# A decoder block on one core: the mixer's splits on VectorE with held rows, candidate sums on GpSimd, the output projection's first tiles side by side, and an ordered norm

## The chip, the cores and the metric

The kernel runs on one core of a Trainium2 chip. The engines have the profile's names: PE is TensorE, DVE is VectorE, ACT is ScalarE, POOL is GpSimd, and SP is SyncE, which here only issues transfers. The metric is the device time of one execution in microseconds, as the median of several runs. The kernel before takes 1098.89 us.

## What is computed

One decoder block on 256 tokens (T) of width 1024 (D), in float32:

```
mod = silu(c) @ w_ada + b_ada              # 6 x 1024: shift1, scale1, gate1, shift2, scale2, gate2
hn  = modulate(rmsnorm(x, norm1_g), shift1, scale1)
qa, ka, va, qi, ki, wi, qb, kb, vb, ga, gb = split(hn @ w_in)
ya  = dsa_attention(qa, ka, va, qi, ki, wi, rel_bias)      # indexer, top 64 keys, softmax
yb  = stick_breaking_attention(qb, kb, vb)
merged = sigmoid(ga) * (ya @ w_proj_a) + sigmoid(gb) * (yb @ w_proj_b)
x   = x + gate1 * (merged @ w_out)
h   = modulate(rmsnorm(x, norm2_g), shift2, scale2)
# peer_ffn: 8 heads; s1, s2 = the top 16 of 128 keys on either half
cand = s1[..., :, None] + s2[..., None, :]                 # candidate sums
top_s, pos = top_k(cand, 16);  g = softmax(top_s)
f   = sum_k g_k * gelu(h . u[e_k]) * v[e_k]
out = rmsnorm(x + gate2 * f, final_g)
```

## The kernel before

**One stream of weights.** A class `Stream` (L58) carries every weight matrix as tiles of 128 x 1024, 512 KB each, in one list `items`: 16 pieces of w1, 29 of w2 (both are w_in), 4 of wpa, 4 of wpb, 8 of wout, 16 of wq, 128 of u and 128 of v. For each piece SP's queue loads `raw` (L78), ACT copies it to `wh` in the reduced format fp32r (L96), and one subtraction raw - wh gives the rest `wl` (L102). That subtraction is called the split. PE multiplies in three products (`three`, L256 to L259): wh with the activations' high part, wh with their low part, wl with the high part. `raw` runs at most 3 pieces ahead (`RAW_AHEAD`) and the splits 2 (`SPLIT_AHEAD`). The third entry of an item says who splits: DVE, POOL, or, where it is None, POOL while `S.share` holds and DVE after that. In the five matrices w2 to wq every odd piece (`i % PS`) goes to POOL, and all of wq.

```
items.append(("mat", A[nm][i], None if nm == "wq" else nc.gpsimd if i % PS else V))
while late and (32 - len(late)) * (45 - VEC0) < 32 * (k - VEC0):
    items.append(late.pop(0))
```

**Rows of the modulation.** The 48 rows of w_ada come in the same list as items of kind "vec": each is loaded as `vraw` by SP's queue and reduced against `cond` by one DVE instruction (L143). 16 are used by the first norm; the other 32 are "late" and are spread over 45 pieces from w2 to wout. They have a pool of three buffers.

**The order.** A scheduler fixes each engine's order at build time from the order of the program and the data dependences. `tc.issue_after(x)` adds the rule that an instruction comes behind instruction x. A late row has no such rule, so it can be moved forward as far as its load allows.

**Mixer.** While the w2, wpa and wpb pieces run, a generator `attention()` adds a step after each piece: the indexer with its top-k on DVE (L420 to L433), the softmax attention and the stick-breaking attention (the DVE results lg L481, lb and lm L536 and L537, ll L541; PE's tiles `at`). Its bias table `brev` is a 1 MB load on POOL's queue (L390), which ACT and POOL then split in two halves (L443, L444). `psm` holds two accumulators "mm".

**Output projection and norm.** Each wpb piece gives m, mh and the rest ml (L662 to L665: two DVE operations, an ACT copy, a DVE subtraction). Then the 8 wout pieces run one after the other: x2 is updated (L679), ACT squares it (L681), POOL sums the squares (L683), and two matmuls with ones (L685) give the norm's sum, then Ln (L234), Exp (L237). Transposes of x2 (L706) save the residual through ACT copies (L708) to DRAM.

**Top-k.** During the 16 wq pieces a head's scores are copied to `s` every second piece (L940), and `topk()` on DVE takes the top 16 of each half (`top16`, L745 to L749: MAX8, FIND_INDEX8, MATCH_REPLACE8, MAX8, FIND_INDEX8). After heads 3 and 7 it adds candidate sums (L796, L798) and takes their top 16. Then e = TV - max (L812), Exp on ACT (L833), lookups, index tables `ix` (L778), three PE transposes `tp` each for the two halves of the tokens (L857). The generators are advanced by budgets: each `yield` names a cost, and a piece grants a number.

**Experts.** 128 u pieces with a Gelu each (L963), while `gates()` on DVE and PE builds the gate matrix; then 128 v pieces; then the last norm.

## Time and profile before

| | before |
|---|---|
| median of 3 runs | 1098.89 us (1098.52 to 1099.18) |
| the profiled execution's own time | 1098.71 us |
| span of its instructions | 1097.0 us |
| busy: PE, DVE, ACT, POOL | 1038.3, 788.4, 576.4, 151.6 us |
| mean granted clock of PE | 0.982 |

The span runs from the first to the last instruction of the execution; its own time has 1.7 us around that. A busy time is the sum of an engine's instructions; PE's is 95% of the span, so 58.7 us are left in which PE does nothing. A row of the profile names line, engine, operation and tiles (out<-in); "[idle before <-releaser]" is the time that the engine stood before it and whose result ended that.

### The profile page before, as it was taken

Reading aid. Unit: us, or ns where it says so; the run is one execution under the profiler, and the core shown is the slowest. Engines: PE = TensorE matmul, PEld = TensorE weight load, DVE = VectorE, ACT = ScalarE, POOL = GpSimd, SP = SyncE. Lnnn points to the kernel's source line nnn. Section 1 sums busy time; section 2 is a strip of 40 time slices with the busy share of each in tenths; the row PEclk is TensorE's granted clock in tenths of the full one; section 3 lists DMA queues with packets and bytes.
Section 4 is the critical chain, followed back from the end, with each engine's and each line's share of the span. In section 5 each row is a group of like instructions: output and inputs, shape, how many; then the busy total and the mean of one; then the engine's idle time right before and its main releaser. Section 6 shows DMA issues by size and latency. Waiting matters only on the chain.

```text
span 1097.0 us, 18990 instructions
## 1 busy us (share of the span) xinstructions
PE 1038.3 (95%) x7237; PEld 952.6 (87%) x7237; DVE 788.4 (72%) x1510; ACT 576.4 (53%) x938; POOL 151.6 (14%) x88
## 2 busy tenths in 40 slices
PE   6997888998994999999999999999999999999996
...
GB/s 299 361 357 216 253 244 133 176 153 195 165 153 101 152 183 172 154 155 173 155 155 167 153 163 183 183 185 241 222 195 195 192 192 192 193 193 193 193 194 72
DMA packets 57949, 208.50 MB, mean 190 GB/s; under 512 B 6673, under 2 KB 6785, under 8 KB 57858
## 3 DMA queue, kind: packets, MB, share of 16 engines
...
q10 hardware_dynamic: 240, 0.08, 0.0%
...
## 4 chain that ended last, share of the span: by engine, by line
PE 80%; DVE 12%; issue 3%; POOL 2%; ACT 1%; DMA 1%; SPq 0%; POOLq 0%; ACTq 0%; DVEq 0%
PE acc L1035 31%; PE mm L257 13%; PE mm L259 13%; PE mm L258 13%; PE gp L897 3%; DVE vraw L143 2%; POOL wl L102 2%; PE a L258 2%; PE a L257 2%; PE a L259 1%; DMA vraw<-in_ada 1%; DVE tmp L747 1%; DVE ll L541 1%; DVE wl L102 1%; DVE cand L798 1%
## 5 line engine op out<-in xcount | busy, mean ns | idle before, releaser
L102 DVE TENSOR_TENSOR wl<-raw,wh 128x1024 fp32r<-128x1024 f32 x285 | 353.1, 1239 | 182.2 <-ACT wh L96 182.1
L96 ACT ACTIVATE wh<-raw 128x1024 fp32r<-128x1024 f32 x333 | 352.9, 1060 | 247.8 <-PE mm L258 144.4
L257 PE MATMUL mm<-hh,wh 128*128 128x256 f32 x1304 | 376.3, 289 | 12.1 <-ACT Xlo L963 9.1
L259 PE MATMUL mm<-hh,wl 128*128 128x256 f32 x1304 | 371.6, 285 | 4.3 <-DVE wl L102 3.6
L258 PE MATMUL mm<-hl,wh 128*128 128x256 f32 x1304 | 371.7, 285 | 0.1
L257 PEld LDWEIGHTS mm<-hh,wh 128*128 128x128 f32 x1304 | 252.6, 194 | 13.7 <-ACT Xlo L963 9.3
L259 PEld LDWEIGHTS mm<-hh,wl 128*128 128x128 f32 x1304 | 252.4, 194 | 4.8 <-DVE wl L102 3.8
L258 PEld LDWEIGHTS mm<-hl,wh 128*128 128x128 f32 x1304 | 252.9, 194 | 0.6 <-issue 0.3
L1035 PE MATMUL acc<-wh,cl 128*128 128x512 f32 x500 | 154.0, 389 | 0.0
L1035 PE MATMUL acc<-wh,ch 128*128 128x512 f32 x500 | 153.9, 389 | 0.0
L1035 PE MATMUL acc<-wl,ch 128*128 128x512 f32 x500 | 153.9, 389 | 0.0
L102 POOL TENSOR_TENSOR wl<-raw,wh 128x1024 fp32r<-128x1024 f32 x48 | 122.5, 2557 | 165.7 <-ACT wh L96 165.7
L1035 PEld LDWEIGHTS acc<-wh,cl 128*128 128x128 f32 x500 | 93.8, 188 | 19.5
L1035 PEld LDWEIGHTS acc<-wl,ch 128*128 128x128 f32 x500 | 93.8, 188 | 19.4
L1035 PEld LDWEIGHTS acc<-wh,ch 128*128 128x128 f32 x500 | 93.8, 188 | 19.5
L1065 POOL TENSOR_TENSOR Xlo<-Xlo 128x512 f32<-128x512 f32 x3 | 3.8, 1282 | 728.5 <-DVE Xlo L1062 727.8
L983 ACT ACTIVATE ch<-Xhi 128x256 fp32r<-128x256 f32 x80 | 33.4, 418 | 96.4 <-PE acc L1035 96.4
L143 DVE CUSTOM_DVE_ANT_0 vraw<-vraw,cond,par 128x1024 f32<-128x1024 f32 x48 | 72.1, 1507 | 2.7 <-DMA vraw<-in_ada 2.7
L985 DVE TENSOR_TENSOR cl<-Xhi,ch 128x256 fp32r<-128x256 f32 x80 | 34.0, 425 | 38.3 <-PE acc L1035 38.3
L983 ACT ACTIVATE ch<-Xlo 128x256 fp32r<-128x256 f32 x48 | 19.9, 418 | 52.9 <-PE acc L1035 52.9
L909 ACT ACTIVATE Xhi<-gp 128x640 f32<-128x640 f32 (+21 forms) x32 | 18.6, 582 | 43.5 <-DVE Xhi L905 42.0
L257 PE MATMUL a<-hh,wh 128*128 128x256 f32 x128 | 34.9, 293 | 3.3 <-ACT hh L252 3.3
...
## 6 DMA issues: line engine op xcount, KB each, us to landing
raw<-in_u SPq DMA_DIRECT2D x128, 512.0 KB, 3.6
raw<-in_v SPq DMA_DIRECT2D x128, 512.0 KB, 4.2
vraw<-in_ada SPq DMA_DIRECT2D x48, 512.0 KB, 5.0
raw<-in_w SPq DMA_DIRECT2D x45, 512.0 KB, 4.8
raw<-in_wq SPq DMA_DIRECT2D x16, 512.0 KB, 3.6
raw<-in_wout SPq DMA_DIRECT2D x8, 512.0 KB, 3.6
raw<-in_wpa SPq DMA_DIRECT2D x4, 512.0 KB, 4.4
raw<-in_wpb SPq DMA_DIRECT2D x4, 512.0 KB, 3.6
```

The source lines that it names most:

```text
L96: self.marka.append(nc.scalar.activation(h, raw, AF.Copy).ins)
L102: ins = arg.tensor_sub(l, raw, h.bitcast(F32)).ins
L143: vins[j] = nc.vector.tensor_tensor_reduce(raw, raw, cond, 1.0, par[:, j:j + 1], OP.mult, OP.add, accum_out=mod[:, j:j + 1]).ins
L257: nc.tensor.matmul(ps, wh, xh, start=start, stop=False, **k)
L258: nc.tensor.matmul(ps, wh, xl, start=False, stop=False, **k)
L259: nc.tensor.matmul(ps, wl, xh, start=False, stop=stop, **k)
L541: nc.vector.tensor_sub(ll, lm, lh.bitcast(F32))
L897: nc.tensor.matmul(gp[:, k], o1[:, k // 2, :, k % 2], o2[q][:, k // 2, :, k % 2], start=q == 0, stop=q == 1)
L909: nc.scalar.activation(t[:, m:, ts], g[:, a + m:a + n], AF.Copy, scale=1.0 / GS)
L983: nc.scalar.activation(ch, c, AF.Copy)
L985: nc.vector.tensor_sub(cl, c, ch.bitcast(F32))
L1035: nc.tensor.matmul(accs[tt * 2 + half], a[:, ts], b[:, half * 512:(half + 1) * 512], start=i == 0 and k == 0, stop=i == 127 and k == 2, sk ...
```

## The change

1. All splits of w2, wpa, wpb, wout and of the first three wq pieces are on DVE (`PS` is gone). The late rows begin after 8 pieces (`VEC0` 8) and each is held behind DVE's last split (`self.low`).
2. The load of `brev` moves from POOL's queue to SP's, and the two copies of it lose one of their two rules of order.
3. The last wpb piece makes m, mh and ml in two halves; the first two wout pieces are multiplied side by side, k 0 to 5 of both, then k 6 and 7 of both.
4. In the norm the transposes of x2's first half stand ahead of the two sums on PE, two of their copies ahead of Ln on ACT, the rest behind Exp.
5. The candidate sums are on POOL, in buffers of their own; their top 16 stand behind all heads in program order. `S.share` ends with the second candidate set. Both Exps stand together; the transposes (`turn`) come later.

```diff
-VEC0 = 0
-PS = 2
+VEC0 = 8
...
         if kind == "vec":
-            arg(raw)
+            with tc.issue_after(self.low) if i >= 4 * ND else nullcontext():
+                arg(raw)
...
-            if arg is nc.gpsimd:
-                self.mark.append(ins)
+            if arg is nc.vector:
+                self.low = ins
...
-            items.append(("mat", A[nm][i], None if nm == "wq" else nc.gpsimd if i % PS else V))
+            items.append(("mat", A[nm][i], None if nm == "wq" and i > 2 else V))
...
-        with tc.issue_after(S.mark[-1]):
-            nc.gpsimd.dma_start(brev, bass.AP(tensor=brow[:].tensor, offset=brow[:].offset,
...
+        nc.sync.dma_start(brev, bass.AP(tensor=brow[:].tensor, offset=brow[:].offset,
...
+        for a, b in ((0, 1), (1, 2)) if i == 3 else ((0, 2),):
+            f = lambda t, j: t[:, j + a:j + b].rearrange("p a b -> p (a b)")
+            c = slice(a * T, b * T)
+            nc.vector.tensor_mul(m[:, c], o[:, c], f(gate[1], 2 * i))
+            nc.vector.tensor_add(m[:, c], m[:, c], f(m1, 2 * i))
+            nc.scalar.activation(f(mh, 2 * i), m[:, c], AF.Copy)
+            nc.vector.tensor_sub(f(ml[i // 2], 2 * i % 4), m[:, c], f(mh, 2 * i).bitcast(F32))
...
+    two = [(S.next(), mm()) for _ in range(2)]
+    for ks in (range(6), range(6, ND)):
+        for (wh, wl), o in two:
+            for k in ks:
+                three(o[:, :T], wh[:, k * P:(k + 1) * P], wl[:, k * P:(k + 1) * P], mh[:, k], mlk[:, k], k == 0,
+                      k == ND - 1)
...
+    turned(0, 0, 0)
+    turned(1, 1, 0)
+    for j in (0, ND - 1):
+        on_pe(ss[:, :T], ones, sq[:, j], start=j == 0, stop=j > 0)
...
+    turned(2, 0, 4, exp)
+    turned(3, 1, 4, exp)
...
-                    cand = tw.tile([P, 4, NC], F32, name="cand")
+                    cand = tk.tile([P, 4, NC], F32, name=f"cand{h}{tt}")
-                    nc.vector.tensor_tensor(cand[:, :, :16], v1[:, :, 0:1].to_broadcast([P, 4, 16]), v2, op=OP.add)
+                    nc.gpsimd.tensor_tensor(cand[:, :, :16], v1[:, :, 0:1].to_broadcast([P, 4, 16]), v2, op=OP.add)
-                        nc.vector.tensor_tensor(
+                        nc.gpsimd.tensor_tensor(
...
-                    for k in range(4):
-                        top16(cand[:, k], NC, TV[tt][:, h - 3 + k], TP[tt][:, h - 3 + k])
-                        yield 950
+                    cands.append((cand, tt, h - 3))
+        for n, (cand, tt, h) in enumerate(cands):
+            S.share = n < 2
+            for k in range(4):
+                top16(cand[:, k], NC, TV[tt][:, h + k], TP[tt][:, h + k])
+                yield 980
...
-        S.share = False
...
-            if tt == 0:
+            if tt:
+                turn(0)
+            else:
                 for a in es:
                     nc.scalar.activation(a, a, AF.Exp)
...
+        yield 3000
+        turn(1)
```

What this does to the engines' orders shows at three places. The first is DVE in the mixer, in the second half of the indexer's top-k (MAX and MATCH_REPLACE; `ISA vraw,mod` is a late row, `wl` a split). Before:

```order
L429 MATCH_REPLACE ism<-m_1176,ism 128x128 [waits DVE_49]
L143 ISA vraw,mod<-vraw,cond,par 128x1024 [waits DMAHW0_49]
L143 ISA mod 128x1
L428 MAX m_1176<-ism 128x8 [waits DVE_49]
L143 ISA vraw,mod<-vraw,cond,par 128x1024 [waits DMAHW2_49]
L143 ISA mod 128x1
L429 MATCH_REPLACE ism<-m_1176,ism 128x128 [waits DVE_49]
L102 TENSOR_TENSOR wl<-raw,wh 128x1024 [waits DMAHW7_49,Activation_49]
L428 MAX m_1176<-ism 128x8 [waits DVE_49]
L143 ISA vraw,mod<-vraw,cond,par 128x1024 [waits DMAHW4_49]
```

and in the change, at the same steps:

```order
L102 TENSOR_TENSOR wl<-raw,wh 128x1024 [waits DMAHW0_49,PE_49,Activation_49]
L428 MATCH_REPLACE ism<-m_1161,ism 128x128 [waits DVE_49]
L143 ISA vraw,mod<-vraw,cond,par 128x1024 [waits DMAHW2_49]
L143 ISA mod 128x1
L427 MAX m_1161<-ism 128x8 [waits DVE_49]
L102 TENSOR_TENSOR wl<-raw,wh 128x1024 [waits DMAHW1_49,Activation_49]
L428 MATCH_REPLACE ism<-m_1161,ism 128x128 [waits DVE_49]
L143 ISA vraw,mod<-vraw,cond,par 128x1024 [waits DMAHW4_49]
L143 ISA mod 128x1
```

Before, several rows stand between two splits; now each split is followed by one row, and the splits are twice as many.

The second place is POOL from the wq pieces on (`wl` a split, `cand` a candidate sum). Before it holds splits alone here:

```order
L239 TENSOR_TENSOR xr_2482<-xr_2482,rr 128x256
L700 DMA gscr<-gr 8x128
L710 DMA xscr<-xts 128x512 x4
L734 DMA sk_2863<-in_sk 128x1024
L734 DMA sk_2864<-in_sk 128x1024
L102 TENSOR_TENSOR wl<-raw,wh 128x1024 x23
L1065 TENSOR_TENSOR Xlo<-Xlo 128x512 x3
```

and in the change the sums of heads 0 to 3 and 4 to 7 stand between the splits:

```order
L102 TENSOR_TENSOR wl<-raw,wh 128x1024 x9
L836 TENSOR_TENSOR cand_3345<-V_2871,V_2873 128x4x24
L836 TENSOR_TENSOR cand_3345<-V_2871,V_2873 128x4x48
L834 TENSOR_TENSOR cand_3345<-V_2871,V_2873 128x4x16
L836 TENSOR_TENSOR cand_3349<-V_2872,V_2874 128x4x24
L836 TENSOR_TENSOR cand_3349<-V_2872,V_2874 128x4x48
L102 TENSOR_TENSOR wl<-raw,wh 128x1024
L834 TENSOR_TENSOR cand_3349<-V_2872,V_2874 128x4x16
L102 TENSOR_TENSOR wl<-raw,wh 128x1024 x6
L836 TENSOR_TENSOR cand_3739<-V_2871,V_2873 128x4x24
L836 TENSOR_TENSOR cand_3739<-V_2871,V_2873 128x4x48
L834 TENSOR_TENSOR cand_3739<-V_2871,V_2873 128x4x16
```

The sums of one token half of four heads are three instructions. On DVE the first MAX over a candidate set now waits for POOL, at this place behind the fourth head (V and I are heads' results, TV and TP those of candidates):

```order
L770 MAX_INDEX I_2878<-V_2874,s_3284 128x8 [waits DVE_49]
L773 MAX_INDEX I_2876<-V_2872,tmp 128x8 [waits DVE_49]
L771 MATCH_REPLACE tmp<-V_2874,s_3284 128x128
L769 MAX TV_2879<-cand_3345 128x8 [waits Pool_49]
L772 MAX V_2874<-tmp 128x8 [waits DVE_49]
L770 MAX_INDEX TP_2881<-TV_2879,cand_3345 128x8 [waits DVE_49]
L773 MAX_INDEX I_2878<-V_2874,tmp 128x8 [waits DVE_49]
L769 MAX TV_2879<-cand_3345 128x8 x2
L770 MAX_INDEX TP_2881<-TV_2879,cand_3345 128x8 [waits DVE_49] x2
L769 MAX TV_2879<-cand_3345 128x8
L769 MAX TV_2880<-cand_3349 128x8 [waits Pool_49]
```

The scheduler has moved the first halves of the candidates' top 16 up to here; the rest of them stands behind the last head.

The third place is ACT around the Exps, at the fourth and fifth u piece (Xlo is the Gelu of a piece). Before:

```order
L963 ACTIVATE Xlo<-mm 128x256
L833 ACT_TABLE_LOAD
L833 ACTIVATE e<-e 128x128
L96 ACTIVATE wh<-raw 128x1024
L963 ACT_TABLE_LOAD
L963 ACTIVATE Xlo<-mm 128x256
L833 ACT_TABLE_LOAD
L833 ACTIVATE e<-e 128x128
L963 ACT_TABLE_LOAD
L963 ACTIVATE Xlo<-mm 128x256
```

and in the change:

```order
L996 ACTIVATE Xlo<-mm 128x256
L96 ACTIVATE wh<-raw 128x1024
L996 ACTIVATE Xlo<-mm 128x256
L874 ACT_TABLE_LOAD
L874 ACTIVATE e<-e 128x128 x2
L996 ACT_TABLE_LOAD
L996 ACTIVATE Xlo<-mm 128x256
```

There are two table loads fewer, and both Exps stand behind the fifth Gelu in place of the fourth and fifth.

## Rows read from the trace of the kernel before

**Rows 1.** The page: PE's busy time with its share of the span and its instructions (part 1), and the groups of DVE's splits and ACT's copies (part 5: count, busy us and mean ns of one, then idle time before them).

```profile
PE 1038.3 (95%) x7237; PEld 952.6 (87%) x7237; DVE 788.4 (72%) x1510; ACT 576.4 (53%) x938; POOL 151.6 (14%) x88
...
L102 DVE TENSOR_TENSOR wl<-raw,wh 128x1024 fp32r<-128x1024 f32 x285 | 353.1, 1239 | 182.2 <-ACT wh L96 182.1
L96 ACT ACTIVATE wh<-raw 128x1024 fp32r<-128x1024 f32 x333 | 352.9, 1060 | 247.8 <-PE mm L258 144.4
```

**Rows 2.** The waits of PE over the span: line, released by which engine's tile and line, us in total, times, longest us.

```profile
PE mm L257 <- ACT Xlo L963: 9.1, 1, 9.1
PE tp L857 <- DVE ix L778: 5.0, 1, 5.0
PE mm L610 <- POOL wl L102: 4.9, 1, 4.9
PE mm L259 <- DVE wl L102: 3.6, 1, 3.6
...
PE at L551 <- DVE ll L541: 3.1, 3, 1.5
PE mm L257 <- ACT hh L252: 2.8, 1, 2.8
...
PE mm L257 <- ACT mh L664: 2.1, 2, 1.1
PE at L685 <- POOL sq L683: 1.9, 1, 1.9
```

**Rows 3.** Six windows: us, then busy us (and count) of PE, PE's weight loads, DVE, ACT and POOL, PE's granted clock, DMA share, GB/s.

```profile
97.62:101.04 3.42, 3.42 (x19) 3.42 (x18) 3.42 (x12) 0.00 (x0) 1.61 (x2) 0.50 0.88 302
111.28:118.10 6.82, 5.91 (x14) 4.65 (x15) 6.82 (x10) 0.76 (x1) 4.17 (x2) 0.50 0.54 168
172.72:176.13 3.41, 3.41 (x19) 3.19 (x17) 3.18 (x6) 3.38 (x6) 0.00 (x0) 0.50 0.76 293
234.16:240.98 6.82, 6.18 (x29) 6.18 (x30) 2.14 (x3) 3.23 (x4) 2.21 (x2) 0.50 0.26 79
343.38:350.21 6.83, 2.87 (x13) 2.87 (x14) 6.83 (x21) 5.80 (x7) 3.00 (x1) 0.50 0.10 13
353.62:360.45 6.83, 3.72 (x18) 3.75 (x19) 6.83 (x15) 0.00 (x0) 2.81 (x2) 0.50 0.51 154
```

**Rows 4.** The same columns for stretches of the mixer, and for that of the output projection and its norm (235 to 262).

```profile
62.00:105.00 43.00, 39.39 (x248) 34.06 (x248) 41.60 (x76) 22.46 (x34) 18.59 (x9) 0.96 0.77 278
105.00:150.00 45.00, 37.10 (x245) 31.65 (x244) 42.01 (x94) 22.48 (x46) 19.59 (x8) 0.92 0.76 257
150.00:195.00 45.00, 39.68 (x311) 34.08 (x309) 38.05 (x76) 33.39 (x63) 9.60 (x4) 0.96 0.51 175
...
235.00:262.00 27.00, 25.09 (x187) 24.63 (x188) 7.39 (x12) 12.84 (x19) 20.24 (x13) 0.89 0.54 155
```

**Rows 5.** From 62 to 195 us: two groups of DVE by line (count, busy us, mean ns of one, idle before), the group of POOL's splits, and single instructions of DVE and POOL from the timeline (start us, us).

```profile
L143 DVE CUSTOM_DVE_ANT_0 vraw<-vraw,cond,par 128x1024 f32<-128x1024 f32 x32 | 51.8, 1621 | 1.8 <-DMA vraw<-in_ada 1.8
L102 DVE TENSOR_TENSOR wl<-raw,wh 128x1024 fp32r<-128x1024 f32 x14 | 20.2, 1441 | 0.7 <-ACT wh L96 0.7
...
L102 POOL TENSOR_TENSOR wl<-raw,wh 128x1024 fp32r<-128x1024 f32 x13 | 37.8, 2913 | 104.5 <-ACT wh L96 104.5
...
61.97 1.28 DVE L143 CUSTOM_DVE_ANT_0 vraw<-vraw,cond,par 128x1024 f32<-128x1024 f32 x1
...
70.55 3.30 DVE L143 CUSTOM_DVE_ANT_0 vraw<-vraw,cond,par 128x1024 f32<-128x1024 f32 x1
...
69.57 3.19 POOL L102 TENSOR_TENSOR wl<-raw,wh 128x1024 fp32r<-128x1024 f32 x1 [1.53 <-ACT wh L96]
```

**Rows 6.** One window with the instructions of line 257 alone (one of a piece's three products): its length, PE's busy time with the count, PE's weight loads, granted clock, DMA share, GB/s.

```profile
195.19:231.00 35.81, 28.24 (x100) 18.91 (x100) 1.00 0.54 162
```

**Rows 7.** The timeline of ACT and of POOL at the second norm.

```profile
258.98 0.40 ACT L681 ACTIVATE sq<-x 128x256 f32<-128x256 f32 x1
...
262.01 0.47 ACT L234 ACTIVATE rr<-at,epsc 128x256 f32<-128x256 f32 x1 [0.17 <-PE at L685]
...
259.19 0.72 POOL L683 TENSOR_TENSOR sq<-sq 128x256 f32<-128x256 f32 x1
```

**Rows 8.** The top-k stage: DVE's candidate sums by line from 297 to 345 us, and the timeline of DVE, ACT and PE around the Exp.

```profile
L798 DVE TENSOR_TENSOR cand<-V,V 128x96 f32<-128x96 f32 (+1 forms) x8 | 6.4, 797 | 0.0
...
L796 DVE TENSOR_TENSOR cand<-V,V 128x64 f32<-128x64 f32 x4 | 1.9, 485 | 0.0
...
344.78 0.27 DVE L812 TENSOR_TENSOR e<-TV 128x128 f32<-128x128 f32 x1
...
344.33 0.31 ACT L833 ACTIVATE e<-e 128x128 f32<-128x128 f32 x1 [9.28 <-DVE e L812]
...
345.61 1.28 ACT L963 ACT_TABLE_LOAD   x1
346.90 0.38 ACT L963 ACTIVATE Xlo<-mm 128x256 f32<-128x256 f32 x1
...
347.34 0.58 PE L257 MATMUL mm<-hh,wh 128*128 128x256 f32 x1 [9.13 <-ACT Xlo L963]
```

**Rows 9.** DMA issues: tiles, queue, count, KB each, median us from issue to landing.

```profile
raw<-in_w SPq DMA_DIRECT2D x45, 512.0 KB, 4.8
...
brev<-brow POOLq DMA_DIRECT2D x1, 1024.0 KB, 9.7
```

More of the change, by code (lines that the diff above doesn't have):

```diff
@@ L673, in body, with residual, ordered, turned @@
     xr = mix.tile([P, ND, T], F32, tag="b8", name="xr2")
-    for i in range(ND + 1):
-        if i < ND:
-            wh, wl = S.next()
-            o = mm()
-            col_piece(wh, wl, ND, mh, mlk, o[:, :T], 0)
-            nc.vector.scalar_tensor_tensor(x2[:, i], o[:, :T], mod[:, 16 + i:17 + i], x2[:, i], op0=OP.mult,
-                                           op1=OP.add)
-            nc.scalar.activation(sq[:, i], x2[:, i], AF.Square)
-            if 0 < i < ND - 1:
-                nc.gpsimd.tensor_add(sq[:, 0], sq[:, 0], sq[:, i])
-        if i >= ND - 1:
-            nc.tensor.matmul(ss[:, :T], ones, sq[:, 0 if i < ND else ND - 1], start=i < ND, stop=i == ND)
+    def residual(i, o):
+        nc.vector.scalar_tensor_tensor(x2[:, i], o[:, :T], mod[:, 16 + i:17 + i], x2[:, i], op0=OP.mult, op1=OP.add)
+        nc.scalar.activation(sq[:, i], x2[:, i], AF.Square)
+        if 0 < i < ND - 1:
+            nc.gpsimd.tensor_add(sq[:, 0], sq[:, 0], sq[:, i])
+    two = [(S.next(), mm()) for _ in range(2)]
[4 more added lines that the diff above has]
+                      k == ND - 1)
+    for i, (_, o) in enumerate(two):
+        residual(i, o)
+    for i in range(2, ND):
+        wh, wl = S.next()
+        o = mm()
+        col_piece(wh, wl, ND, mh, mlk, o[:, :T], 0)
+        residual(i, o)
+    xscr = scr.tile([2, P, D], F32, name="xscr")
+    gscr = scr.tile([8, P], F32, name="gscr")
+    xts = mix.tile([P, 4, 512], F32, tag="a8", name="xts")
+    def ordered(*a, **k):
+        with tc.issue_after(done[0]):
+            done[0] = nc.tensor.transpose(*a, **k).ins
+    def turned(q, tt, d0, behind=None):
+        tp = at()
+        for e in range(4):
+            ordered(tp[:, e * P:(e + 1) * P], x2[:, d0 + e, tt * P:(tt + 1) * P], ident)
+        with tc.issue_after(behind) if behind else nullcontext():
+            nc.scalar.activation(xts[:, q], tp, AF.Copy)
+    turned(0, 0, 0)
+    turned(1, 1, 0)
+    for j in (0, ND - 1):
+        on_pe(ss[:, :T], ones, sq[:, j], start=j == 0, stop=j > 0)
     nc.gpsimd.tensor_scalar(xr[:, 0], x2[:, 0], g1[:, 8:9], 0.0, op0=OP.mult, op1=OP.add)
     r = rstd_of(ss[:, :T], table, first=xr[:, 0])
+    exp = xins[-1]
     for dt in range(ND):
@@ L690, in body @@
     tap("x2", x2)
-    behind = S.mark[-1]
-    xscr = scr.tile([2, P, D], F32, name="xscr")
-    gscr = scr.tile([8, P], F32, name="gscr")
     tp = at()
-    nc.tensor.transpose(tp[:8, :P], mod[:, 40:48], ident)
+    ordered(tp[:8, :P], mod[:, 40:48], ident)
     gr = mw.tile([8, P], F32, tag="ex", name="gr")
-    nc.scalar.activation(gr, tp[:8, :P], AF.Copy)
-    with tc.issue_after(behind):
-        nc.gpsimd.dma_start(gscr, gr)
-    xts = mix.tile([P, 4, 512], F32, tag="a8", name="xts")
-    for q in range(4):
-        tt, d0 = divmod(q * 512, D)
-        tp = at()
-        for e in range(4):
-            nc.tensor.transpose(tp[:, e * P:(e + 1) * P], x2[:, d0 // P + e, tt * P:(tt + 1) * P], ident)
-        xt = xts[:, q]
-        nc.scalar.activation(xt, tp, AF.Copy)
-        with tc.issue_after(behind):
-            nc.gpsimd.dma_start(xscr[tt, :, d0:d0 + 512], xt)
+    with tc.issue_after(exp):
+        nc.scalar.activation(gr, tp[:8, :P], AF.Copy)
+    turned(2, 0, 4, exp)
+    turned(3, 1, 4, exp)
+    with tc.issue_after(S.mark[-1]):
+        nc.gpsimd.dma_start(gscr, gr)
+        for q, (tt, d0) in enumerate(((0, 0), (1, 0), (0, 512), (1, 512))):
+            nc.gpsimd.dma_start(xscr[tt, :, d0:d0 + 512], xts[:, q])
     pats.close()
@@ L779, in lookup, with turn @@
         yield 970
+    def turn(tt):
+        tp = sps.tile([P, 512], F32, tag="s", name="tp")
+        for k in range(3):
+            nc.tensor.transpose(tp[:, k * P:(k + 1) * P], ix[tt][k], ident)
+        ts = slice(tt * P, (tt + 1) * P)
+        nc.scalar.activation(i1T[:, ts], tp[:, :P], AF.Copy)
+        nc.scalar.activation(i2T[:, ts], tp[:, P:2 * P], AF.Copy)
+        gt = tk.tile([P, P], F32, name=f"gt{tt}")
+        nc.scalar.activation(gt, tp[:, 2 * P:3 * P], AF.Copy, scale=GS)
+        nc.scalar.activation(gh[:, ts], gt, AF.Copy)
+        nc.vector.tensor_sub(gl[:, ts], gt, gh[:, ts])
     def topk():
+        cands = []
         for h in range(8):
@@ L854, in topk @@
             yield 600
-            tp = sps.tile([P, 512], F32, tag="s", name="tp")
-            for k in range(3):
-                nc.tensor.transpose(tp[:, k * P:(k + 1) * P], ix[tt][k], ident)
-            ts = slice(tt * P, (tt + 1) * P)
-            nc.scalar.activation(i1T[:, ts], tp[:, :P], AF.Copy)
-            nc.scalar.activation(i2T[:, ts], tp[:, P:2 * P], AF.Copy)
-            gt = tk.tile([P, P], F32, name=f"gt{tt}")
-            nc.scalar.activation(gt, tp[:, 2 * P:3 * P], AF.Copy, scale=GS)
-            nc.scalar.activation(gh[:, ts], gt, AF.Copy)
-            nc.vector.tensor_sub(gl[:, ts], gt, gh[:, ts])
-            yield 400
+        yield 3000
+        turn(1)
+        yield 400
     X, late = [(Xlo, 0, S0)], {}
```

13 lines of the change are left out of this document (4 added, 9 removed).

## Prediction

> **What bounds the kernel now.** I read the page's busy times first: TensorE (PE) works 1038.3 of 1097.0 us [rows 1], so the kernel is PE-bound, and another engine matters only where PE stands still for it. The waits of PE come second [rows 2]: two large ones behind the top-k work (9.1 for a Gelu on ScalarE, 5.0 for a DVE index table), 4.9 for a GpSimd subtraction, 3.6 for a DVE one, and a few of 1.9 to 2.8. Those ahead of the first stream pieces and after the last stay as they are; the change reaches only waits between 62 and 360 us. Third, the windows at half clock: the granted clock reads 0.50 (1.2 of 2.4 GHz) in six stretches [rows 3], each beginning within or soon after a wait. There PE was busy 3.42, 5.91, 3.41, 6.18, 2.87 and 3.72 us; at full clock half of it, so the stretches cost 6.4 in the mixer (the first three), 3.1 at the output projection and 3.3 in the top-k stage. A closed wait can therefore give back more than itself.
>
> Fourth, the reason for the mixer's waits. From 62 to 195 us DVE is busy 41.60, 42.01 and 38.05 us [rows 4]: 121.7 of 133, 92%, so what PE waits for there is mostly DVE's place in line. Part of that is not work. A late row takes 1.28 us alone, and 3.30 where it starts at 70.55 inside a GpSimd subtraction (69.57 to 72.76): it ends as that ends [rows 5]. The means show the same: 32 rows at 1.62 and 14 splits at 1.44 where the whole kernel's mean is 1.24 [rows 1, 5]. Over 1.28 and 1.24 that is 32 x 0.34 + 14 x 0.20 = 13.7 us in which DVE waits for GpSimd's two-input work.
>
> **The change, part by part.** The sum stands against the profiled execution's own time, 1098.71 us (0.2 under the median of the runs, 1098.89).
>
> *A, mixer.* At stake are PE's idle times, 43 - 39.39, 45 - 37.10 and 45 - 39.68 = 16.8 us [rows 4], and 6.4 of clock: 23.2. GpSimd's 13 splits of these 133 us come over to DVE: +13 x 1.24 = 16.1. All 32 late rows ran here [rows 5]; the new spread has 18 due by the end of w2's 29 pieces (32/37 for each piece from the ninth on), so 14 leave this stage: -14 x 1.28 = -17.9. The waiting beside GpSimd, -13.7, goes with its cause, but for two casts of the bias table that stay on GpSimd. DVE then holds 121.7 + 16.1 - 17.9 - 13.7 = 106.2 us of the same 133, 80%: it can keep ahead of PE. A held row waits behind one split already due, and nothing but the rows behind it waits for it. What stays: splits that meet the two bias casts (some 2 us), and the attention chains' own length (PE waited up to 1.5 at a time for them [rows 2]), where DVE is asked for the result and PE has nothing else left; with a little clock 5.7 of the 23.2. I take **17.5**. Bounds: 8 (only the waits that name a split, 3.6 + 4.9) and 23.
>
> *B, output projection.* A wait of 2.1 in two parts for mh [rows 2], and 3.1 of clock: 5.2. A piece lasts 35.81 us / 12.5 = 2.87 [rows 6], since 100 products, 8 to a piece, run in that window. With two tiles side by side PE has k 0 to 5 of two tiles, 4.3 us, before it needs the last products of the projection, where it had 2.15. But the DVE chain that delivers them now carries two more splits and two late rows, 2 x 1.24 + 2 x 1.28 = 5.0, less two or so of the GpSimd waits of 2.0 (3.30 - 1.28). That is 2.15 of cover for some 1 to 3 of delay: I take **0.5**, bounds 0 and 5.2.
>
> *C, norm.* PE waited 1.9 for GpSimd's last sum [rows 2], which ran at 259.19, a subtraction ahead of it on GpSimd; the square of the last tile came at 258.98 + 0.40 = 259.38, and Ln at 262.01 [rows 7]. Without the subtraction the sum is there before the square; two copies (on ScalarE now ahead of Ln) put Ln at about 260.5: **1.5**, bounds 0.5 and 3 (all that could go of the 2.8 that PE then waits for hh).
>
> *D, top-k.* Waits 9.1 + 5.0, clock 3.3: 17.4. The 9.1 is a queue: ScalarE stands at an Exp until 344.33, for DVE's last e subtractions, the second of them at 344.78; behind the Exp stand the split copy, a table load and the Gelu that frees PE's accumulator at 347.3 [rows 8]. The twelve candidate sums hold DVE 6.4 + 1.9 = 8.3 us [rows 8]. Off DVE they could bring the second e to 336.5. A part is lost where DVE, now ahead, waits for a head's scores (they come every two pieces) or for GpSimd's sums; of the 8.3 I take 6, so e at 338.8. Both Exps now stand one piece later, behind the fifth Gelu. Two Exps of 0.31, a load of 1.28 and a Gelu of 0.38 bring the next accumulator free at 341.0, and PE wants it one piece after 347.34 - 9.13 = 338.21, at 341.1. So it just closes. The 5.0 wait was for transposes put right behind the index table; 16 pieces later, some 46 us, nothing is late. I take **16.5**, bounds 6 and 17.4. On GpSimd a sum is not shown; by its 1024-wide subtraction of 2.91 [rows 5] scaled to 64, 96 and 192 columns it is 0.2 to 0.5, by its 256-wide sum, 0.72 [rows 7], at most that. Three sums are 1.0 to 2.2. GpSimd has a split of 2.91 every second piece, 5.7, so 2.8 to spare: hidden.
>
> By a rule that speaks against this part (the Trainium skill, *GPSIMD Engine Reference*, 4.1 Engine selection) a two-input add belongs on VectorE and takes about twice as long on GpSimd. By that rule and DVE's 8.3 the sums would be 16.6 in all, 4.2 for three, more than one slack holds, and a split would come 1.4 late, which the piece of lead still covers.
>
> *Costs taken at nothing.* The 1 MB table load, 9.7 us [rows 9], goes from GpSimd's queue to SP's: it stands between weight loads that run three pieces ahead; if that cover were gone, about 1 us. Three wq splits go to DVE, busy 7.39 of 27 us at 235 to 262 [rows 4].
>
> Two table loads go (4 to 2). The row shows a load of 1.28 at 345.61 and the Gelu at 346.90, at once [rows 8]. The Trainium skill (*ScalarE: Activation LUTs*, What ACT_TABLE_LOAD costs) gives a switch another 1.38 us of drain; by that PE would wait some 1.4 longer here, about 1064, but the rows have no room for a drain.
>
> Sum: 17.5 + 0.5 + 1.5 + 16.5 = 36.0, so 1098.7 - 36.0 = **1063 us**.
>
> **The rivals.**
> 1. *DVE stays full in the mixer.* All splits on one engine, and attention's chains beside them: for it, 13 splits come in, and the rows that leave may catch up early; against it, 106.2 of 133. It would save some 6 in place of 17.5: 1074. Chance 0.13.
> 2. *The Exps stay late.* DVE asks for the sums as soon as head 3 is through, and they may stand behind GpSimd's splits (2.91 each): DVE then stands too, the Exps stay late, and D gives 6, its lower bound (the 5.0 of the transposes and some clock): 1073. Chance 0.12.
> 3. *Everything fills.* 23 + 5 + 3 + 17 = 48: 1050. Chance 0.08.
> 4. *The stream starves (slower).* SP's queue is in order. A held row keeps its buffer, the next row's load waits for that buffer at the head of the queue, and weight loads behind it wait too. A piece then takes landing 4.8 [rows 9], copy 1.06 and split 1.24 [rows 1], 7.1 in place of 2.87; over ten pieces +42, against the 36 above: 1105. It decides when DVE lags by more than the three loads ahead, 8.6 us. Against it: DVE at 80%. Chance 0.03.
> 5. *The waits only move.* Mixer and top-k give back what they gain (PE reaches the next late result sooner) and the time stays near 1098. Chance 0.02.
>
> **How the numbers follow.** The forecast has 0.62, with its own range of 1055 to 1072 from A's and D's nearer bounds. The range for eight in ten takes in cases 1 and 2 and part of case 3: 1052 to 1079. A measurement of this kernel can tell about 0.2% (2.2 us) from no change; faster by more than that: 0.62 + 0.13 + 0.12 + 0.08 = 0.95; within it 0.02; slower 0.03.
>
> **What would show it.** Right: in the mixer no row or split over 2 us on DVE except beside the two bias casts, PE idle between 62 and 231 us under 6, half-clock stretches there gone or one left; both Exps together within 1 us of 339 in the old time scale, no wait over 2 us on either Gelu or transposes. The first norm Ln 1.5 earlier after the last projection piece. Wrong: waits on attention's lm, ll, lg as long as before with DVE over 90% (case 1); top16 of a candidate set waiting for GpSimd (case 2); PE waits on DVE splits whose release traces to a landed raw tile (case 4).

## The result, and the profile after

The change takes 1067.03 us (median of 6 runs, 1065.65 to 1068.88) against 1098.87: a ratio of 0.9714, 95% interval 0.97 to 0.9729, or 31.8 us. The forecast was 1063, range 1052 to 1079. The profiled execution of the change takes 1066.10 us (span 1064.3), 32.6 less than that of before.

Where the 32.6 come from shows when each stage's first product starts on PE. Each line is the length from one such start to the next, in us:

| stretch on PE | before | after | difference |
|---|---|---|---|
| start to the first product of w2 | 65.41 | 65.10 | -0.3 |
| w2, wpa, wpb (term A) | 164.03 | 147.33 | -16.7 |
| wout, first to last product (B) | 28.33 | 27.81 | -0.5 |
| last wout product to the first of wq (C) | 7.96 | 5.84 | -2.1 |
| wq to the last score | 55.85 | 56.32 | +0.5 |
| last score to the first v product (D) | 417.03 | 403.64 | -13.4 |
| v and the end | 358.34 | 358.26 | -0.1 |

The waits of PE after the change (line, released by, us in total, times, longest). The 9.1 at the Gelu [rows 2] is 2.3 (Xlo), the 5.0 at the transposes is gone, the 4.9 and 3.6 at the mixer's splits are one of 2.1. New is the first row, 2.7 for the residual x.

```profile
PE mm L257 <- DVE x L678: 2.7, 1, 2.7
...
PE at L291 <- DVE lm L536: 2.4, 1, 2.4
PE mm L257 <- ACT Xlo L996: 2.3, 1, 2.3
PE mm L609 <- DVE wl L102: 2.1, 1, 2.1
```

Between 62 and 360 us four stretches at half clock are left of six [rows 3], in the columns of that group:

```profile
129.64:133.05 3.41, 3.41 (x16) 2.84 (x15) 3.41 (x10) 3.41 (x10) 0.00 (x0) 0.51 0.38 155
221.84:225.25 3.41, 3.29 (x15) 3.29 (x16) 3.41 (x6) 0.81 (x2) 3.05 (x2) 0.50 0.91 311
245.70:249.11 3.41, 3.03 (x14) 3.03 (x15) 3.38 (x10) 2.21 (x5) 2.79 (x6) 0.51 0.80 288
324.24:327.65 3.41, 3.41 (x16) 3.41 (x17) 3.41 (x5) 2.04 (x3) 0.00 (x0) 0.50 0.16 36
```

The mixer and the stretch behind it, in the columns of [rows 4]. DVE is busy 114.1 of 133 us up to 195 (86%), and 39.4 of 40 from 195 to 235: the load is not gone, it has moved to the output projection.

```profile
62.00:105.00 43.00, 40.90 (x260) 34.76 (x259) 36.62 (x70) 23.57 (x35) 7.70 (x5) 1.00 0.70 235
105.00:150.00 45.00, 42.09 (x321) 36.38 (x320) 40.03 (x104) 30.30 (x64) 0.29 (x1) 0.96 0.67 222
150.00:195.00 45.00, 44.88 (x380) 42.11 (x379) 37.43 (x70) 33.35 (x56) 0.00 (x0) 1.00 0.69 231
195.00:215.00 20.00, 17.67 (x146) 17.12 (x145) 19.97 (x30) 8.24 (x9) 0.00 (x0) 1.00 0.85 300
215.00:235.00 20.00, 17.35 (x135) 17.13 (x135) 19.41 (x29) 9.29 (x14) 6.04 (x5) 0.91 0.73 234
```

DVE's splits and rows from 62 to 195 us, and single instructions of DVE and of GpSimd (POOL). The means of 1.44 and 1.62 [rows 5] are 1.29 and 1.36. The split at 95.28 and the row at 98.97 end 1.1 us after GpSimd's two bias casts (98.65 behind 97.56, 101.99 behind 100.91): each stands until the cast has ended and then does its own work.

```profile
L102 DVE TENSOR_TENSOR wl<-raw,wh 128x1024 fp32r<-128x1024 f32 x32 | 41.4, 1294 | 10.6 <-ACT wh L96 10.6
L143 DVE CUSTOM_DVE_ANT_0 vraw<-vraw,cond,par 128x1024 f32<-128x1024 f32 x21 | 28.6, 1360 | 0.0
...
95.28 3.37 DVE L102 TENSOR_TENSOR wl<-raw,wh 128x1024 fp32r<-128x1024 f32 x1
...
98.97 3.02 DVE L143 CUSTOM_DVE_ANT_0 vraw<-vraw,cond,par 128x1024 f32<-128x1024 f32 x1
...
95.16 2.40 POOL L443 TENSOR_TENSOR yl<-brev,yh 128x1024 fp32r<-128x1024 f32 x1 [4.64 <-ACT yh L442]
97.53 3.38 POOL L443 TENSOR_TENSOR b<-brev,b 128x1024 fp32r<-128x1024 f32 x1
```

At the output projection, DVE and PE. The third tile needs the first one's accumulator, which the residual (L678) frees; that stands on DVE behind a late row and a split, 2.65 us too late for PE. (x2 means that both residuals are in the row.)

```profile
219.09 1.28 DVE L143 CUSTOM_DVE_ANT_0 vraw<-vraw,cond,par 128x1024 f32<-128x1024 f32 x1
...
220.29 1.22 DVE L102 TENSOR_TENSOR wl<-raw,wh 128x1024 fp32r<-128x1024 f32 x1
221.43 0.87 DVE L678 SCALAR_TENSOR_TENSOR x<-mm,mod,x 128x256 f32<-128x256 f32 x2
...
221.96 0.58 PE L257 MATMUL mm<-mh,wh 128*128 128x256 f32 x1 [2.65 <-DVE x L678]
```

ACT at the norm. Two copies stand ahead of Ln, as said, and Ln starts 0.9 after the last square has ended; before it was 2.6 after it [rows 7].

```profile
241.45 0.40 ACT L679 ACTIVATE sq<-x 128x256 f32<-128x256 f32 x1
241.76 1.07 ACT L712 ACTIVATE xts<-at 128x512 f32<-128x512 f32 x2
242.71 0.47 ACT L234 ACTIVATE rr<-at,epsc 128x256 f32<-128x256 f32 x1
```

The top-k stage: DVE, ACT, PE, and two sums on POOL. Between the two e stands a split of 1.22, and the second Exp waits 1.40 for it. The next Gelu starts 1.30 after its table load, with no time between; a sum on GpSimd takes 0.30 to 0.51.

```profile
320.07 0.30 DVE L852 TENSOR_TENSOR e<-TV 128x128 f32<-128x128 f32 x1
...
320.43 1.22 DVE L102 TENSOR_TENSOR wl<-raw,wh 128x1024 fp32r<-128x1024 f32 x1
321.79 0.29 DVE L852 TENSOR_TENSOR e<-TV 128x128 f32<-128x128 f32 x1
...
322.11 0.31 ACT L874 ACTIVATE e<-e 128x128 f32<-128x128 f32 x1 [1.40 <-DVE e L852]
322.43 1.28 ACT L996 ACT_TABLE_LOAD   x1
323.73 0.38 ACT L996 ACTIVATE Xlo<-mm 128x256 f32<-128x256 f32 x1
...
324.16 0.54 PE L257 MATMUL mm<-hh,wh 128*128 128x256 f32 x1 [2.27 <-ACT Xlo L996]
...
304.92 0.51 POOL L836 TENSOR_TENSOR cand<-V,V 128x192 f32<-128x192 f32 x1 [0.62 <-DVE V L772]
305.63 0.30 POOL L834 TENSOR_TENSOR cand<-V,V 128x64 f32<-128x64 f32 x1 [0.20 <-DVE V L772]
```

### The profile page after: what moved, and what is told of

It reads as the page before. It is cut to its first block, busy times and chain, and to the rows that moved or that the text cites. A ratio compares the mean times of both kernels' runs of the same rounds, so it can differ in the third digit from the quotient of the medians.

```text
span 1064.3 us, 18966 instructions
## 1 busy us (share of the span) xinstructions
PE 1029.5 (97%) x7237; PEld 945.5 (89%) x7237; DVE 785.1 (74%) x1527; ACT 570.5 (54%) x935; POOL 82.6 (8%) x71
## 4 chain that ended last, share of the span: by engine, by line
PE 83%; DVE 10%; issue 3%; ACT 2%; DMA 1%; POOL 0%; SPq 0%; ACTq 0%; DVEq 0%; POOLq 0%
PE acc L1068 32%; PE mm L257 14%; PE mm L258 14%; PE mm L259 14%; PE gp L930 3%; DVE wl L102 3%; DVE vraw L143 1%; PE a L258 1%; PE a L259 1%; PE a L257 1%; DMA vraw<-in_ada 1%; ACT wh L96 1%; PE at L291 1%; DVE tmp L771 1%; DVE ism L428 1%
## 5 line engine op out<-in xcount | busy, mean ns | idle before, releaser
L102 DVE TENSOR_TENSOR wl<-raw,wh 128x1024 fp32r<-128x1024 f32 x313 | 385.4, 1232 | 179.7 <-ACT wh L96 179.7
L1068 PEld LDWEIGHTS acc<-wl,ch 128*128 128x128 f32 x500 | 93.9, 188 | 19.5
L1068 PEld LDWEIGHTS acc<-wh,cl 128*128 128x128 f32 x500 | 93.9, 188 | 19.4
L1068 PEld LDWEIGHTS acc<-wh,ch 128*128 128x128 f32 x500 | 93.8, 188 | 19.5
L143 DVE CUSTOM_DVE_ANT_0 vraw<-vraw,cond,par 128x1024 f32<-128x1024 f32 x48 | 64.3, 1344 | 1.1 <-DMA vraw<-in_ada 1.0
L102 POOL TENSOR_TENSOR wl<-raw,wh 128x1024 fp32r<-128x1024 f32 x20 | 47.8, 2399 | 14.8 <-ACT wh L96 14.8
L942 ACT ACTIVATE Xhi<-gp 128x640 f32<-128x640 f32 (+25 forms) x32 | 17.7, 553 | 48.1 <-DVE Xhi L938 48.1
```

Of the source, the lines that this page charges most:

```text
L102: ins = arg.tensor_sub(l, raw, h.bitcast(F32)).ins
L143: vins[j] = nc.vector.tensor_tensor_reduce(raw, raw, cond, 1.0, par[:, j:j + 1], OP.mult, OP.add, accum_out=mod[:, j:j + 1]).ins
L942: nc.scalar.activation(t[:, m:, ts], g[:, a + m:a + n], AF.Copy, scale=1.0 / GS)
L1068: nc.tensor.matmul(accs[tt * 2 + half], a[:, ts], b[:, half * 512:(half + 1) * 512], start=i == 0 and k == 0, stop=i == 127 and k == 2, sk ...
```

## The experiments

Each is an edit of the changed kernel where not said otherwise. Line numbers move by one where an edit takes a line out. Ratios are to the kernel before, run beside it (medians of 1099.1 to 1101.4), with the 95% interval. The first product of w2 comes up to 2.6 us later in some of these runs than in the change, though their edits touch nothing ahead of it; so where two times are close, the text goes by the stretches of the table above, read from each run's trace.

**Every odd split on GpSimd again.**

```diff
-None if nm == "wq" and i > 2 else V
+None if nm == "wq" else nc.gpsimd if i % 2 else V
```

> The changed kernel (1067.0) with every odd split of w2 to wout, and all of wq, on GpSimd again; the late rows stay spread and held. My theory (the mixer's 16.7 us come from taking two-input work off GpSimd as well as from the rows that left): rows and splits on DVE are lengthened again beside GpSimd's subtractions (means near 1.6 for rows and 1.4 for splits, where the change has 1.36 and 1.29), PE waits again for GpSimd's wl, and half or more of the mixer's gain is lost: 1075 to 1082. Rival (the new spread of the rows did it alone, who splits is indifferent): 1065 to 1069.

Measured 1080.44, ratio 0.9813 (0.978 to 0.9845). The rival falls: the rows' new spread with splits on both engines keeps less than two thirds of the gain. Of the 13.4 lost, 9.6 are in the mixer (156.96) and 3.3 in the norm (9.11). DVE is busy only 103 of the 133 us up to 195, 77%, and PE still loses 9.1 there. DVE's rows and splits are longer again, by line from 62 to 195:

```profile
L143 DVE CUSTOM_DVE_ANT_0 vraw<-vraw,cond,par 128x1024 f32<-128x1024 f32 x20 | 29.5, 1490 | 0.0
L102 DVE TENSOR_TENSOR wl<-raw,wh 128x1024 fp32r<-128x1024 f32 x16 | 22.3, 1394 | 12.4 <-ACT wh L96 12.4
```

**Rows free.** All splits on DVE, rows over all 45 pieces and not held.

```diff
-VEC0 = 8
+VEC0 = 0
-            with tc.issue_after(self.low) if i >= 4 * ND else nullcontext():
-                arg(raw)
+            arg(raw)
```

> The changed kernel with the late rows spread over all 45 pieces and not held, as before; all splits stay on DVE. My theory: 11 or so more rows of 1.28 come back into 62 to 195 us, DVE stands near 120 of 133 us busy, attention's results come late again and PE waits 8 to 12 us more in the mixer, while at the output projection the 2.65 wait for the residual and 1.5 of clock go: 1069 to 1076. Rival (only the GpSimd work mattered, rows find room anywhere): 1061 to 1065, faster than the change, since the output projection is then free of rows.

Measured 1065.45, ratio 0.9675 (0.9652 to 0.9699). My expectation falls; the time lies just above the rival's range. The windows:

```profile
62.00:105.00 43.00, 42.34 (x277) 36.36 (x275) 40.33 (x75) 24.81 (x36) 7.12 (x4) 1.00 0.79 284
105.00:150.00 45.00, 39.40 (x284) 34.28 (x285) 43.46 (x105) 26.98 (x55) 1.92 (x3) 0.96 0.73 246
150.00:195.00 45.00, 43.86 (x355) 39.28 (x354) 38.98 (x83) 33.40 (x62) 0.00 (x0) 1.00 0.70 223
195.00:215.00 20.00, 20.00 (x172) 20.00 (x172) 15.00 (x18) 11.41 (x11) 0.00 (x0) 1.00 0.62 183
```

DVE is busy 122.8 of 133 us in the mixer, 92%, the same share as before the change; still PE loses 7.4 us there and not 16.8, and none from 195 to 215. A wait of 4.1 for attention's lg appears, as expected, but the wait for the residual and its clock are gone, and the stage's end comes out the same. So the busy share that I had taken as the reason was not the main one. It is not without a price, though: the mixer takes 150.20, 2.9 more than with held rows, and the output projection 22.44, 5.4 less. Held rows move a wait from the one to the other.

**Candidate sums on DVE.**

```diff
-nc.gpsimd.tensor_tensor(cand[...
+nc.vector.tensor_tensor(cand[...
```

> The changed kernel with the twelve candidate sums on DVE again; their top 16 stay behind the heads. My theory: the sums cost DVE 3 us undisturbed to 8.3 beside GpSimd's splits, and all of it lands ahead of e, so the wait for the Gelu at 321.9 grows from 2.3 to 5 to 10 and the clock falls for longer: 1070 to 1077. Rival (the later top 16 and the Exps' place did it, the sums' engine is indifferent): 1065 to 1069.

Measured 1071.13, ratio 0.9732 (0.9707 to 0.9757): the time is in the expected range, the place is not the expected one. PE's wait and two of the sums on DVE (64 columns each):

```profile
PE mm L259 <- DVE wl L102: 4.7, 1, 4.7
...
311.39 1.53 DVE L834 TENSOR_TENSOR cand<-V,V 128x64 f32<-128x64 f32 x1
...
313.74 2.42 DVE L834 TENSOR_TENSOR cand<-V,V 128x64 f32<-128x64 f32 x1
```

Two 64-wide sums take 1.53 and 2.42 on DVE beside GpSimd's splits. The wait shows up at a DVE split, which stands in the same queue, and not at the Gelu, for which PE no longer waits. From the last score to the first v product it takes 406.87, 3.2 more than in the change: that much of D's 13.4 hangs on the sums' engine. The other ten come with the rest of part 5 (top 16 behind the heads, Exps together, transposes later), which no run takes apart.

**Output projection one tile after the other**, last projection piece in one part.

```diff
-    two = [(S.next(), mm()) for _ in range(2)]
...
-    for i in range(2, ND):
+    for i in range(ND):
-        for a, b in ((0, 1), (1, 2)) if i == 3 else ((0, 2),):
+        for a, b in ((0, 2),):
```

> The changed kernel with the output projection's tiles one after the other and the last projection piece in one part. My theory: PE waits 2 to 4 for the last mh again, but the first tile's accumulator is freed earlier, so that the 2.65 wait for the residual shrinks by about as much: 1066 to 1069. Rival (side by side is worth its 2.15 us of cover): 1069 to 1072.

Measured 1065.18, ratio 0.9675 (0.9653 to 0.9698), below both ranges: side by side gives nothing, and here it costs. The longer wait for mh that my theory had did not come; it is 0.7, as in the change. The wait for the residual is

```profile
PE mm L257 <- DVE x L678: 0.9, 4, 0.2
```

in place of 2.7, and no stretch of half clock is left in that stage; from the first to the last product it takes 25.64 in place of 27.81. (In the six runs with tiles side by side and held rows this is 26.6 to 29.1; the half-clock stretch comes in four of them.) Two tiles that end together ask for both residuals at once, ahead of the third tile; one after the other, the first residual has a piece's time.

**The same where no row stands at the output projection**: free rows, tiles one after the other; the edits of the two runs with those names, together.

```diff
-VEC0 = 8
+VEC0 = 0
...
-    two = [(S.next(), mm()) for _ in range(2)]
```

> The kernel of the run with free rows (all splits on DVE, rows spread over 45 pieces and not held, 1065.5) with the output projection's first two tiles one after the other and the last projection piece in one part. There no row stands in DVE's way at the output projection, and side by side PE had no wait there. Theory A (side by side is worth its cover of 2.15 once DVE is free there): waits of 1.5 to 2.5 for mh return, with or without a stretch of half clock: 1066.5 to 1069.5. Theory B (mh comes in time anyway without GpSimd's splits): no wait over 0.5, 1064.5 to 1066.

Measured 1065.17, ratio 0.9673 (0.9654 to 0.9692). Theory B: PE has no wait over 0.1 us from the first to the last product of the stage, as with side by side, and from the first product of w2 to the last of wout both take 172.6. The waits for mh before [rows 2] go when GpSimd has no splits and no held row stands there.

**Three u splits on GpSimd**, so that the two e follow each other.

```diff
-            S.share = n < 2
+            S.share = True
...
             es.append(e)
+        S.share = False
```

> The changed kernel with three splits of the first u pieces on GpSimd in place of DVE, so that no split stands between the last top 16 and the two e (one of 1.22 at 320.43 in the change). My theory: the second e comes 1.2 earlier, PE's wait for the Gelu falls from 2.27 to about 1.0, while the clock may fall as before: 1065 to 1067, the wait in the trace decides. Rival (the wait is for the first Exp's table or for ScalarE's order, not for the second e): the wait stays at 2.2 to 2.3 and the time at 1066 to 1068.

Measured 1072.36, ratio 0.973 (0.9708 to 0.9751), slower than both theories had it. The trace is of an execution of 1069.18. PE's waits:

```profile
PE mm L259 <- DVE wl L102: 3.5, 1, 3.5
...
PE mm L257 <- ACT Xlo L997: 1.3, 1, 1.3
```

The wait for the Gelu fell to 1.3, as my theory said, but DVE's lookups now ran beside two of these splits (DVE and POOL):

```profile
323.48 2.92 DVE L798 TENSOR_TENSOR eq<-eq 128x1024 bf16<-128x1024 bf16 x1
326.32 2.42 DVE L879 TENSOR_SCALAR m<-TP 128x128 uint32<-128x128 uint32 x1
...
323.43 5.24 POOL L102 TENSOR_TENSOR wl<-raw,wh 128x1024 fp32r<-128x1024 f32 x2 [4.53 <-ACT wh L96]
```

The sum of 1024 columns took 2.92 and a TENSOR_SCALAR 2.42. In the changed kernel, with no GpSimd split beside them, they are

```profile
327.63 0.70 DVE L798 TENSOR_TENSOR eq<-eq 128x1024 bf16<-128x1024 bf16 x1
328.23 0.23 DVE L878 TENSOR_SCALAR m<-TP 128x128 uint32<-128x128 uint32 x1
```

DVE came late with a later split, and PE waited 3.5 for it.

**The bias table's casts on DVE.**

```diff
-                        nc.gpsimd.tensor_sub(bl, b, bh.bitcast(F32))
+                        nc.vector.tensor_sub(bl, b, bh.bitcast(F32))
```

> The changed kernel with the two subtractions of the bias table (2.40 and 3.38 on GpSimd) on DVE, so that GpSimd does no two-input work in the mixer. My theory (a DVE two-input operation beside a GpSimd one lasts until that ends): no split or row in the mixer over 1.5 us, where one split took 3.37 and one row 3.02; DVE spends 2 x 1.24 itself and saves 3.9; PE's wait of 2.09 for the split there falls below 1: 1064 to 1067. Rival (the split was late for another reason, the queue of the indexer): the wait stays at 2 or grows, 1067 to 1069.

Measured 1061.17, ratio 0.9633 (0.9614 to 0.9652): 5.9 us faster than the change, more than expected. The mixer takes 141.24, 6.1 less. On DVE:

```profile
99.25 1.21 DVE L443 TENSOR_TENSOR b<-brev,b 128x1024 fp32r<-128x1024 f32 x1
100.38 1.42 DVE L143 CUSTOM_DVE_ANT_0 vraw<-vraw,cond,par 128x1024 f32<-128x1024 f32 x1
...
101.73 1.21 DVE L102 TENSOR_TENSOR wl<-raw,wh 128x1024 fp32r<-128x1024 f32 x1
```

The casts cost DVE 2.4 us, the row and the split beside them are short, and PE's wait there fell from 2.09 to 0.27. More came from behind: the attention waits of 0.55 and 2.36 fell to 0.32 and 0.15 and the half-clock stretch at 129.64 is gone.

**The norm's order as before.**

```diff
-    turned(0, 0, 0)
-    turned(1, 1, 0)
-    for j in (0, ND - 1):
-        on_pe(ss[:, :T], ones, sq[:, j], start=j == 0, stop=j > 0)
+    for j in (0, ND - 1):
+        nc.tensor.matmul(ss[:, :T], ones, sq[:, j], start=j == 0, stop=j > 0)
...
```

> The changed kernel with the second norm's order as before: transposes of x2 not ordered on PE, one copy to xts and the copy to gr ahead of Ln, the rest where the scheduler puts it; GpSimd stays free of splits. My theory (Ln comes later by the copies ahead of it): the step from the last product of the output projection to the first of wq grows from 5.84 by 0.5 to 1.5, 1067 to 1069. Rival (GpSimd free of splits did all of the norm's 2.1, the order nothing): 5.6 to 6.0, 1066 to 1067.5.

Measured 1067.95, ratio 0.9699 (0.9678 to 0.972), not to be told from the change by time. In the trace the step from the last wout product to the first of wq is 6.17, between the two theories: of the 2.1 gained, 0.3 are the order. The other 1.8 go with GpSimd free of splits; the run with the splits alone, the next one, has 6.17 as well.

**Splits alone, on the kernel before.** Rows, tiles, norm, sums and Exps as before.

```diff
-None if nm == "wq" else nc.gpsimd if i % PS else V
+None if nm == "wq" and i > 2 else V
-            if arg is nc.gpsimd:
-                self.mark.append(ins)
+            self.mark.append(ins)
```

> One part alone on the kernel before: the splits of w2, wpa, wpb, wout and of the first three wq pieces on DVE; rows free over 45 pieces, output projection, norm's order, sums and Exps as before (the bias table's load and casts keep a rule of order behind a split). Theory A (GpSimd's two-input work was the cause in mixer, output projection and norm; rows, tiles and order add nothing): waits of 9.1 and 5.0 in the top-k stay, everything ahead of wq comes as in the change or earlier, so 1098.9 - 16.7 - 0.5 - 2.1 + 0.5 = 1080, range 1077 to 1083. Theory B (rows had to leave the mixer as well): 1087 to 1095.

Measured 1083.38, ratio 0.9844 (0.9816 to 0.9872): theory A, though just above its range. The mixer takes 149.93 here and wout 23.13. From the first product of w2 to the first of wq that makes 179.2, against 200.3 before and 181.0 in the change: the splits alone bring all that A, B and C gained, and held rows, tiles and order together add nothing there. What is missing lies ahead: the first product of w2 comes at 70.73 and not at 65.41. The bias table's load, with no GpSimd split ahead of it, starts at 22.2 here; the next run shows what that does.

**The bias table's load on GpSimd's queue.**

```diff
-        nc.sync.dma_start(brev, bass.AP(
+        nc.gpsimd.dma_start(brev, bass.AP(
```

> The changed kernel with the bias table's load on GpSimd's queue again. The prediction took the queue for nothing, 1 us at most: 1066 to 1068, the mixer's waits as in the change. Rival (on SP's queue the 1 MB stands ahead of weights, or on GpSimd's it lands earlier or later and moves the casts): over 1.5 us either way.

Measured 1072.65, ratio 0.9747 (0.9719 to 0.9775): the rival, 5.6 slower. The intervals of the two ratios overlap, but each of the six times (1070.3 to 1074.0) is above each of the change's six, and the trace shows where the loss is. The load's issue on GpSimd in this run:

```profile
21.78 0.96 POOL L389 DMA_DIRECT2D brev<-brow  x1 [3.97 <-DMA brow<-rbs]
```

Nothing on GpSimd's queue holds it any more, so it starts at 21.78, where the DMA engines are full with the first weights and rows (landing 10.8); before it stood behind a split, at 67.06. The window from 32 to 40 us, first of this run, then of the change:

```profile
32.00:40.00 8.00, 4.97 (x29) 4.90 (x29) 5.55 (x10) 3.26 (x5) 0.00 (x0) 0.79 1.01 402
```

```profile
32.00:40.00 8.00, 8.00 (x69) 8.00 (x68) 6.78 (x9) 4.89 (x9) 0.00 (x0) 1.00 1.00 381
```

PE waits 3.0 for an activation's low part, which stands on DVE behind three rows of the first norm; DVE waits 0.95, 0.74 and 1.31 for their loads. The clock falls, and w2 begins 5.2 later. In the change the load has its place in SP's queue, behind weights and rows, and starts at 63.3. That it is the start and not the queue by itself that counts is argued from the trace; no run starts it early on SP's queue.

**Free rows and DVE casts together**, by the edits shown above.

```diff
-VEC0 = 8
+VEC0 = 0
...
-                        nc.gpsimd.tensor_sub(bl, b, bh.bitcast(F32))
+                        nc.vector.tensor_sub(bl, b, bh.bitcast(F32))
```

> The changed kernel with free rows (1065.5) and the bias table's two casts on DVE (5.9 off the change by itself). If the two gains come from different places (casts: the split at 101.7 and attention's waits behind it; free rows: the output projection), they add up but for the attention wait of 2.4 that both touch: 1058 to 1061. If DVE, with 32 rows and the casts in the mixer, is full there, attention's results come late and it is 1062 to 1066, no better than the casts alone.

Measured 1060.79, ratio 0.9642 (0.9615 to 0.9669): at the end of the first range, but not to be told from the casts alone (1061.17). The gains do not add: with free rows, waits of 0.90 for a split and 1.44 for lg come back in the mixer, which takes 145.93 against 141.24 with the casts alone, and the output projection takes 22.44 against 26.63.

**One u split on GpSimd**, on top of that.

```diff
+            S.extra += n == 2
...
-                arg = nc.gpsimd if self.share else nc.vector
+                arg = nc.gpsimd if self.share or self.extra else nc.vector
+                self.extra = 0 if not self.share else self.extra
```

> The kernel with free rows and DVE casts (1060.8) with just one split of the u stage, the one of 1.23 at 315.94 between the two e, on GpSimd; the next ones stay on DVE, so that no GpSimd split runs beside the lookups. My theory (the run with three such splits lost its gain to DVE work beside GpSimd, not to the earlier e): the wait for the Gelu falls from 2.27 to about 1.3 as there, no lookup over 1.3 us, no new wait for a DVE split: 1059 to 1060.5. Rival (any change of the place of splits there makes a later one late): a wait for wl of 1 to 3.5 appears, 1061 to 1065.

Measured 1059.09, ratio 0.9625 (0.96 to 0.965), as expected: no lookup over 1.24, no wait for a split over 0.2 there, and no half clock in that stage. Its median is the lowest of all and its interval clear of the change's; it overlaps that of the run without this edit. There the stretch from the last score to the first v product shows the gain, 401.64 in place of 403.65.

```profile
PE mm L257 <- ACT Xlo L997: 1.3, 1, 1.3
```

## Why the prediction was right, and where not

In all 36.0 were forecast and 32.6 measured; most of the difference is in D.

**A, mixer: right in size, half right in reason.** 17.5 forecast, 16.7 measured. That sharing two-input work between DVE and GpSimd was the main cause is shown three times: 9.6 us of the mixer come back with GpSimd's splits, 6.1 more go with the last two casts, and splits alone on the kernel before bring the stage to 149.93 of 164.03. The runs with the splits do not part DVE's waiting from GpSimd's own late results (4.9 of the waits [rows 2] name a GpSimd split); in the run with the casts it is parted: PE waited there for a split of DVE's own, held up by the split of 3.37 and the row of 3.02 ahead of it. The other half of the step, that 14 rows must leave so that DVE falls to 80%, fails as the reason: the change has DVE at 86% and loses 5.1 in PE up to 195, the run with GpSimd's splits has it at 77% and loses 9.1, and with all rows back it is at 92%, as before, and PE loses 7.4 in place of 16.8. The share averages work that may wait with work that may not. The held rows are worth 2.9 in the mixer (4.7 with the casts on DVE), and the output projection gives as much back. The residual of some 2 us at the bias casts was named; that it led to the attention waits and the clock behind them, 6 in all, was not. One row was misread: the late row at 70.55 [rows 5] does not end with GpSimd's subtraction, at 72.76, but 1.1 later, at 73.85. The 13.7 goes by means and is not touched by that.

**B, output projection: 0.5 forecast and 0.5 measured, by other parts, so by luck.** The old waits of 2.1 for mh are 0.7 in the change and nothing with free rows. They went with GpSimd's splits, not with the tiles side by side, which are worth nothing (one after the other: same time with free rows, 1.9 faster by the medians with held ones). What I had as a delay of mh by 1 to 3 came as the wait of 2.65 for the residual, since rows and splits stand ahead of it: a wait that the step did not name, with a half-clock stretch behind it. Two more, of 0.6 for an accumulator and 1.1 for wh, come just ahead of the first wout product and count in A's stretch; they too are gone with free rows.

**C, norm: 1.5 forecast, 2.1 measured**, 1.8 of it with GpSimd free of splits, 0.3 from the order.

**D, top-k: 16.5 forecast, 12.9 measured** (13.4, less 0.5 in wq, where the clock falls once more). The transposes no longer wait, the Exps stand together, and three sums took 1.2 on GpSimd, within the forecast. The term that was mis-sized is the second e. Counted from the last score (its place is the sum of the table's stretches up to it) it started at 23.2 before (344.78 - 321.58) and at 19.4 in the change (321.79 - 302.40): 3.8 earlier, where the sum took 6. PE wanted the accumulator when the forecast said, 19.5 after the last score; it waited 2.3, and the clock cost 1.7. From the fourth head's scores to the second e, the sums had held up DVE's queue by 7.4, not 8.3, since their busy times overlap with the instructions behind them. In the change DVE stands 2.2 more there for scores and sums, which the forecast allowed for, and the split of 1.22 between the two e, which it did not name, takes 1.1; the top 16 are as many instructions as before. Moving that split took 0.9 off the 2.3 (the last run). That the rest is the overlap and small differences is worked out from the two traces and not shown by a run. That ScalarE would need a drain behind its table load (the Trainium skill, *ScalarE: Activation LUTs*, What ACT_TABLE_LOAD costs: 1.38 us more) is not seen: the load starts at 322.43 and the Gelu at 323.73.

**Costs at nothing.** The bias table's load on SP's queue costs nothing, as said; that without it the change would have lost 5.6 was overlooked, since the split that held it was removed by the same change.

**The rivals.** DVE stays full and would cost 11: it stayed full in the free-rows run, and the mixer took 2.9 more. Exps stay late: 2.3 of 9.1 is left, and the top 16 waited for GpSimd once, 0.85. The stream starves: PE waits for no landed tile from w2 on. Everything fills: 32.6 of 48. The waits only move: they do so from the mixer to the output projection, by a small part. None of the five came as a whole.

**The signs.** Met: no row or split in the mixer over 2 us but beside the two casts, one half-clock stretch left there, Ln 1.8 earlier after the last wout product. Missed: PE idle 6.8 us from the first product of w2 to the first of wout and not under 6, the second Exp 1.7 behind the first and 2.3 behind 339 in the old time scale (counted from the last score), and a wait of 2.3 for the Gelu.
